# A hybrid decoder trunk on one core: whole-array transposes for DeltaNet's meta rows, and GLA score products in pieces of 24

## The chip, the cores and the metric

One core of a Trainium2 chip runs the whole program. The metric is device time in microseconds, the median over runs; less is better. TensorE (PE) multiplies matrices, VectorE (DVE) and ScalarE (ACT) work element by element, GpSimd (POOL) helps, and SyncE (SP) issues most of the transfers. Each engine takes its instructions in the order in which the program lists them.

## The reference

The reference is one layer of a language model with three token mixers side by side, for 512 tokens of width 2048 and 16 learned meta tokens ahead of them:

```
h    = pad(rms_norm(concat(meta, x), norm_w))
proj = h @ w_in                                # 2048 x ~7600 columns, split among three mixers
qkv  = silu(causal_depthwise_conv(dq, dk, dv))
o_dn  = gated_delta_rule(l2norm(q), l2norm(k), v, decay, beta)   # 6 heads x 128, chunked
o_gla = gla(q / 8, k, v, key-dim gate)                            # 5 heads, dk 64, dv 128
o_fox = softmax(q k^T / sqrt(128) + c_t - c_s, causal) v          # 5 heads x 128
each branch: times silu(z), the first two after a head norm
out  = rms_norm(x + concat(o_dn, o_gla, o_fox) @ w_out, final_norm_w)[:, 16:]
```

All of it is in float32. In GLA the score of query i and key j has a decay for each of the 64 key channels, `exp(g_i - g_j)`.

## The kernel before, in words

**Data and stages.** Tokens lie along the free axis, 16 meta tokens first (T = 528). Large products are made from operands split exactly into two parts (`hi`, `lo`), three products for each. The stages follow one another on TensorE:

1. The input projection. Nearly all of it runs as 18 pairs of 128-column blocks, each pair as seven products instead of eight (a Strassen-like scheme). `loads` fetches the weights of a pair as four tiles `a`, `sums` adds them on VectorE into `s` and back into `a`, `operand` splits each into `hp` (ScalarE) and `lp` (VectorE), `mm_pair` multiplies into the banks `px`, and `evac_pair` and `store` bring the result into the tile `u`. Pairs of DeltaNet's dk, dv and dq alternate with pairs of the other two mixers.
2. For each dk, dv and dq head, `conv` writes the convolved row into `cv`, and `token_rows` (line 725) turns it, so that tokens lie on partitions: four 128x128 transposes into one PSUM bank (`pkdk`, `pkdv`, `pkdq`), ScalarE's copies out of it into `u` (for dk after a pass of squares), a store; then, for dk and dv, a further transpose of the 16 meta columns into the same bank (line 742), ScalarE's one or two operations on it into `cv`, and a store into `kms` or `vms`. The further transpose overwrites what the copies read, so it waits for them. After it, bank, row `cv` and, with both heads of the pair done, tile `u` are given back.
3. DeltaNet, GLA and forgetting attention (Fox), woven into the last 16 single blocks of the input projection (`pbgq`, `pbgz`, `pbfq`, `pbfz`), which fill TensorE while the mixers wait for other engines.
4. The output projection (`po`, `ps`, `pz`) and the last norm.

**GLA's score products.** The 128x128 block of scores is cut in levels s = 64, 32, 16, 8, 4, 2, 1, 0. The levels go in four groups, (64, 32), (16, 8), (4, 2), (1, 0), for each of three pairs of heads (the third has one head). `level_operands` makes for each level a decayed key `kx` and query `qx` on VectorE and ScalarE. They lie in two sets of buffers, which come free when the products of the group are out. `gla_levels` (line 1377) lists the products of a group: 24 for (64, 32) and 64 for each of the others, in the third pair 12 and 32. They are small (64 rows by 64 or 32 columns) and write the banks `pss`. The list is handed to the planner in pieces of `CH` products (line 1401).

**The planner.** What runs when is worked out while the program is built. Every step is a generator (a chain) that yields operations; `Weave` keeps a clock for each engine from a table of costs, and lists the operations in the order in which its clocks let them start. Each engine then runs in that order. Chains have a priority, and on TensorE a slack in us, added to the time at which their operation is ready: 3.0 for `token_rows` (priority -0.1, line 854), 0.25 by default; the main stream of products has priority 0.25 (line 2047). On its clock a transpose costs 0.11 us and a small product 0.028.

TensorE's operations are of two classes. `light` are those with few columns, rows or weights (line 189). At a change of class the clock adds 0.1 us into light and 0.2 us back (`emit`, line 262). Which class is to come is settled by these lines, where `ran` is the time in the present class; after that, an operation of the wanted class that is ready on the clock is taken ahead of the one that priority and slack would choose:

```
op.light = key == "P" and (n < 64 or ins[0].shape[0] < P or ins[0].free_size() < P)
if self.mode:                                   # light now
    other = ran + (sum(o.dur for o in c[3]) if c[3][0].light else 0.0) > LIGHT      # 1.5
else:
    other = ran >= HEAVY                                                            # 1.5
kind = self.mode != other
if c[3][0].light != kind:
    like = [x for x in self.chains if ... x[3][0].light == kind and x[4] <= t + NEAR]   # 0.05
```

So a transpose of 16 columns is light, and one of 128 columns is not.

Of the kernel before, what the change touches and what calls it, by code (L numbers as in the profile page):

```python
# [18 lines left out]
P = 128  # L19
D = 2048  # L20
KT = D // P
NM = 16
# [66 lines left out]
NXP, SQP, NSL = -0.6, 0.0, 1.5  # L89
LP, LSL = 0.1, 1.0  # L90
EXTRA = ()
NOP, CH, CD = 0, 32, 32
WP, AOP, HDP = 1.0, -0.6, 0.0
EARLY_KP = (3, 4)
STK, KOS, OS0, OSN, OSP = (3, 4, 6, 7), 3, 1, 2, 0.1
# [267 lines left out]
def tile_hybrid_trunk(ctx, tc, xT, xtok, mtok, w_gate, w_first, w_in, w_out, consts, lmask, fin_w, out):  # L363
    nc = tc.nc
    ctx.enter_context(nc.allow_low_precision("operands are split exactly into two parts"))
    W = Weave(tc)
    V, A, G, PE, SP = (Engine(k, e) for k, e in zip("VAGPS", (nc.vector, nc.scalar, nc.gpsimd, nc.tensor, nc.sync)))
# [24 lines left out]
    ident = one((P, P), "ident")  # L392
# [332 lines left out]
    def token_rows(key, c, u):  # L725
        what, h = key
        g, j = divmod(h, H)
        blocks = [slice(b * P, (b + 1) * P) for b in range(NB)]
        dst, dstm, scale, acc_, ev = {"dk": (kds, kms, dl, nks, e_gate), "dv": (vps, vms, br, None, e_keys[g]),
                                      "dq": (None, None, None, nqs, e_gate)}[what]  # L730
        yield ev
        pk = yield Get(bank_s, f"pk{what}{h}", keep=2)
        yield [PE.transpose(pk[:, s], c[:, NM + s.start : NM + s.stop], ident) for s in blocks]
        if acc_ is not None:
            for b, s in enumerate(blocks):
                yield A.activation(u[:, s], pk[:, s], AF.Square, accum_out=acc_[:, b, h : h + 1])
        if dst is not None:
            for b, s in enumerate(blocks):
                yield A.activation(u[:, s], pk[:, s], AF.Copy, scale=scale[:, b, h : h + 1])
            yield SP.dma_start(out=dst[g].rearrange("p (b j) d -> p j b d", j=H)[:, j],  # L740
                               in_=u[:, :S].rearrange("p (b d) -> p b d", b=NB))
            yield PE.transpose(pk[:NM, :P], c[:, 0:NM], ident)
            m = c[:NM, P : 2 * P]
            if acc_ is not None:
                yield A.activation(m, pk[:NM, :P], AF.Square, accum_out=acc_[:NM, NB, h : h + 1])
            yield A.activation(m, pk[:NM, :P], AF.Copy, scale=scale[:NM, NB, h : h + 1])
            yield SP.dma_start(out=dstm[g][:, j], in_=m)
        bank_s.give(pk)
        row_s.give(c)
        sp_of(key).set()  # L750
        if what != "dv":
            {"dk": e_nk, "dq": e_nq}[what][h].set()
# [20 lines left out]
    pairs = [Pair(i) for i in range(len(PAIRS))]  # L773
# [68 lines left out]
    def store(p, n, u):  # L842
        yield VT(out=u, in0=u, in1=rstd, op=ALU.mult)
        key = p.keys[n]
        if key[0] in ("gz", "fz"):
            spill[key] = drp.tile([P, S], F32, name=f"sp{key[0]}{key[1]}")
            yield from silu_row(u[:, NM:], key, spill[key], True)
            sp_of(key).set()
        elif key[0] in CONV:
            c = yield Get(row_s, f"cv{p.i}{n}")  # L850
            yield from conv(u, key, c, u)
            if key[0] != "dv":
                yield spilled(key, c)
            W.go(token_rows(key, c, u), -0.1, f"rows{key[0]}{key[1]}", 3.0)
        else:
            yield spilled(key, u)
            sp_of(key).set()
# [68 lines left out]
    def give(t, *ss):  # L926
        for s in ss:
            if id(t) in s.held:
                s.give(t)
# [625 lines left out]
    def finish(i, z, s):  # L1555
        if i // 2 in ST:
            e_z[i].set((z, s))
            return
        if s:
            yield e_split  # L1560
        pools, keep = ((op_s, s), (KO, 3)) if s else (op_s, 0)
        hi = yield Get(pools, f"oh{i}", (P, S), F32R, keep)
        lo = yield Get(pools, f"ol{i}", (P, S), F32R, keep)
        dparts[i] = hi, lo
        if s is None:
            h_, l_ = (t.rearrange("p (b d) -> p b d", b=NB) for t in (hi, lo))
        else:
            h_, l_, z_ = hi, lo, z[:, :S]
        yield A.copy(h_, z_ if s else z)
        yield VT(out=l_, in0=z_ if s else z, in1=h_.bitcast(F32), op=ALU.subtract)  # L1570
        if s:
            s.give(z)
        for b in range(NB):
            oparts[i, b] = hi[:, b * P : (b + 1) * P], lo[:, b * P : (b + 1) * P]
        e_head[i].set()
# [156 lines left out]
    def phase_d():  # L1732
        yield e_c
        W.go(residual(), 0.0, "residual")
        for h in range(DN_HEADS):
            W.go(finish(h, gs[h // H].kd.rearrange("p (b j) d -> p j b d", j=H)[:, h % H], None), -0.05, f"split{h}")
        yield tuple(e_head[h] for h in range(DN_HEADS))
        e_split.set()
        for g in range(2):
            for q in range(3):  # L1740
                r_s.lend(gs[g].kd[:, 4 * q : 4 * q + 4, :].rearrange("p n d -> p (n d)"))
        for kp in ST:
            W.go(seven_heads(kp), HDP, f"heads{kp}")
        W.go(seven_loads(), -0.3, "sloads")
        W.go(seven_operands(), -0.45, "sops")
        yield tuple(e_z[i] for kp in ST for i in (2 * kp, 2 * kp + 1)) \
            + tuple(e_head[i] for kp in LATE for i in (2 * kp, 2 * kp + 1)) + (e_fin,)
        sweep()
        e_d.set()

    def sweep():
        w_s.move(d_s)
        f_s.move(d_s)
# [46 lines left out]

    def out_sums():
        for i, (cp, kp) in enumerate((cp, kp) for cp in range(2) for kp in ST):
            p, q = pairs[OS0 + OSN * i : OS0 + OSN * i + 2]
            yield p.done[1]
            t = osum[cp, ST.index(kp)]
            (a, b), (c, d) = (tuple(w_out[2 * cp + n, kp][:, k * S : (k + 1) * S] for k in range(2)) for n in range(2))
            for n, w in ((5, c), (7, d), (6, d), (4, b)):
                yield SP.dma_start(out=t[:, SUMS.index(n)], in_=w)
            for n, w, ev in ((5, a, p.done[6]), (7, c, p.done[7]), (6, t[:, SUMS.index(5)], q.done[1]),
                             (4, t[:, SUMS.index(6)], q.done[6])):  # L1810
                yield ev
                yield G.dma_start(out=t[:, SUMS.index(n)], in_=w, accum_op=ALU.add)
        e_osum.set()
# [4 lines left out]
    def seven_loads():  # L1818
        for s in SEV:
            for i, (n, kp) in enumerate((n, kp) for n in ORDER for kp in ST):  # L1820
                    if i == 6:
                        yield tuple(e_head[2 * kp] for kp in ST)
                    t = yield Get((r_s, d_s) if i > 5 or s.cp else r_s, f"w{s.cp}{kp}{n}", (P, S), F32,
                                  (0, KR) if i > 5 or s.cp else 0)
                    sm = osum[s.cp, ST.index(kp)]
                    raw = {1: (0, 0), 2: (0, 1), 3: (1, 1)}.get(n)
                    src = w_out[2 * s.cp + raw[0], kp][:, raw[1] * S : (raw[1] + 1) * S] if raw else sm[:, SUMS.index(n)]
                    yield SP.dma_start(out=t, in_=src)
                    s.src[kp, n].set(t)

    def seven_operands():
        yield e_d
        for s in SEV:
            for n in ORDER:
                if n == ORDER[NOP]:
                    yield tuple(e_head[2 * kp] for kp in ST)
                for kp in ST:
                    src = yield s.src[kp, n]
                    hi = yield Get(d_s, f"wh{s.cp}{kp}{n}", (P, S), F32R)
                    lo = yield Get(d_s, f"wl{s.cp}{kp}{n}", (P, S), F32R)  # L1840
                    yield A.copy(hi, src)
                    yield VT(out=lo, in0=src, in1=hi.bitcast(F32), op=ALU.subtract)
                    give(src, r_s, d_s)
                    s.op[n, kp].set((hi, lo))
# [37 lines left out]
    def residual():  # L1882
        for cc in range(4):
            for tb in range(4):
                yield OUT[cc][min(1 + tb // 2, len(OUT[cc]) - 1)].op
                acc[tb, cc] = yield Get(op_s, f"acc{cc}{tb}", (P, S), F32)
                yield SP.dma_start(out=acc[tb, cc], in_=xtok[tb * P : (tb + 1) * P, cc * 512 : (cc + 1) * 512])
            e_res[cc].set()
# [165 lines left out]
    W.go(phase_b(), 0.0, "phaseB")  # L2054
    W.go(phase_c(), 0.0, "phaseC")
    W.go(phase_d(), 0.0, "phaseD")
    W.go(final_weights(), 0.2, "finw")
    W.run()
# [57 lines left out]
```

## Time and profile before

| what | value |
|---|---|
| median of 3 runs | 963.39 us (963.23 to 964.7) |
| the profiled execution, its own time | 963.21 us |
| its span, first to last instruction | 961.4 us |
| mean granted TensorE clock | 0.997 |
| TensorE busy, by the record | 948.3 us |
| VectorE, ScalarE, GpSimd busy | 738.5, 581.2, 66.1 us |
| bytes moved | 167.20 MB, mean 174 GB/s |

Between the span and the execution's own time lie 1.8 us. The matrix records overlap: a product of 264 columns is recorded as 0.28 us long, and the next starts 0.12 us after it. So a time on TensorE is read from start to start and not from the length of a record. In the profile `x64` behind small products counts two records for each float32 product. All lines of the kernel carry the line of one helper (L285), so work is told apart by the names of tiles.

### The profile page before, as it was taken

The numbers are of one execution on the slowest core, as the hardware profiler recorded it, in microseconds if no ns is written. First come the engines' busy times: TensorE is split into PE (matmuls) and PEld (weight loads), VectorE is DVE, ScalarE is ACT, GpSimd is POOL, SyncE is SP. The second block draws the span as 40 slices with busy tenths as digits, with TensorE's granted clock in tenths as the row PEclk, the third lists the DMA queues.
The fourth block names the chain that finished last, engine by engine and source line by source line (L and its number), as shares of the span: only waits on it lengthen the run. The fifth ranks groups of instructions, "written<-read, shape, count | busy, mean of one in ns | idle before, by whom it ended". The sixth has DMA issues, their size and how long they took to land.

```text
span 961.4 us, 19098 instructions
## 1 busy us (share of the span) xinstructions
PE 948.3 (99%) x7283; PEld 844.6 (88%) x7283; DVE 738.5 (77%) x1308; ACT 581.2 (60%) x1243; POOL 66.1 (7%) x118
## 2 busy tenths in 40 slices
PE   9999999999999999999999999999999999999996
PEld 7888999999999999999987898878778878888885
DVE  7976888888888887888883665785765886887774
ACT  7855466757756575754432775848737756355445
POOL 0000101001101010110001110101010100000000
PEclk9999999999999999999999999999999999999998
DMA  9933647557786668783178545334323364565414
GB/s 348 367 121 132 162 136 219 163 183 197 198 239 151 208 150 224 183 241 93 67 255 297 167 95 172 135 101 146 117 95 111 130 213 154 195 230 174 151 59 176
DMA packets 92145, 167.20 MB, mean 174 GB/s; under 512 B 16253, under 2 KB 36477, under 8 KB 92052
## 3 DMA queue, kind: packets, MB, share of 16 engines
q1 hardware_dynamic: 87156, 157.31, 49.8%
q0 software_dynamic: 4608, 8.39, 6.3%
q8 instruction: 57, 0.93, 0.4%
q14 instruction: 36, 0.29, 0.1%
q10 hardware_dynamic: 288, 0.27, 0.1%
HBM read 142.33 MB, written 40.39 MB: 190 GB/s over the span
## 4 chain that ended last, share of the span: by engine, by line
PE 94%; DMA 2%; ACT 2%; DVE 1%; issue 0%; DVEq 0%; POOL 0%; SPq 0%; ACTq 0%; POOLq 0%
PE px L285 38%; PE po L285 10%; PE ps L285 8%; PE pbfz L285 6%; PE pz L285 6%; PE pbfq L285 5%; PE pbgz L285 5%; PE pbdz L285 2%; PE pks L285 2%; PE pfa L285 1%; PE pg L285 1%; PE pfw L285 1%; PE pss L285 1%; PE pbgq L285 1%; PE pgo L285 1%; DMA sc<-ab 1%
## 5 line engine op out<-in xcount | busy, mean ns | idle before, releaser
L285 DVE SCALAR_TENSOR_TENSOR lp<-a,hp 128x1024 fp32r<-128x1024 f32 x90 | 110.5, 1228 | 37.6 <-ACT hp L285 35.2
L285 ACT CAST hp<-a 128x1024 fp32r<-128x1024 f32 x90 | 94.5, 1049 | 72.4 <-PE px L285 45.4
L285 PE MATMUL px<-xh,hp 128*128 128x264 f32 x432 | 123.6, 286 | 0.0
L285 PE MATMUL px<-xh,lp 128*128 128x264 f32 x432 | 122.9, 285 | 0.0
L285 PE MATMUL px<-xl,hp 128*128 128x264 f32 x432 | 122.9, 285 | 0.0
L285 PE MATMUL px<-tah,hp 128*128 128x264 f32 x288 | 84.0, 292 | 0.0
L285 PE MATMUL px<-tbh,hp 128*128 128x264 f32 x288 | 82.5, 287 | 0.0
L285 PE MATMUL px<-tbh,lp 128*128 128x264 f32 x288 | 82.1, 285 | 0.0
L285 PE MATMUL px<-tah,lp 128*128 128x264 f32 x288 | 82.0, 285 | 0.0
L285 PE MATMUL px<-tbl,hp 128*128 128x264 f32 x288 | 81.9, 284 | 0.0
L285 PE MATMUL px<-tal,hp 128*128 128x264 f32 x288 | 81.8, 284 | 0.0
L285 PEld LDWEIGHTS px<-xh,hp 128*128 128x128 f32 x432 | 81.4, 188 | 0.0
L285 PEld LDWEIGHTS px<-xh,lp 128*128 128x128 f32 x432 | 81.3, 188 | 0.0
L285 PEld LDWEIGHTS px<-xl,hp 128*128 128x128 f32 x432 | 81.2, 188 | 0.0
L285 ACT CAST hp<-s 128x1024 fp32r<-128x1024 f32 x36 | 37.8, 1049 | 29.7 <-PE px L285 19.8
L285 PEld LDWEIGHTS px<-tbh,hp 128*128 128x128 f32 x288 | 54.3, 189 | 0.1
L285 PEld LDWEIGHTS px<-tbl,hp 128*128 128x128 f32 x288 | 54.3, 189 | 0.0
L285 PEld LDWEIGHTS px<-tah,hp 128*128 128x128 f32 x288 | 54.3, 188 | 0.1
L285 PEld LDWEIGHTS px<-tal,hp 128*128 128x128 f32 x288 | 54.3, 189 | 0.0
L285 PEld LDWEIGHTS px<-tah,lp 128*128 128x128 f32 x288 | 54.2, 188 | 0.0
L285 PEld LDWEIGHTS px<-tbh,lp 128*128 128x128 f32 x288 | 54.2, 188 | 0.0
L285 DVE SCALAR_TENSOR_TENSOR lp<-s,hp 128x1024 fp32r<-128x1024 f32 x36 | 44.0, 1222 | 8.4 <-ACT hp L285 8.4
(406 smaller groups left out, 2639.5 us busy)
## 6 DMA issues: line engine op xcount, KB each, us to landing
a<-in_w_in SPq DMA_DIRECT2D x72, 512.0 KB, 6.3
osum<-in_w_out SPq DMA_DIRECT2D x32, 256.0 KB, 6.2
o<-in_w_out SPq DMA_DIRECT2D x16, 512.0 KB, 3.6
kd<-osum SPq DMA_DIRECT2D x26, 256.0 KB, 3.6
kd<-in_w_out SPq DMA_DIRECT2D x21, 256.0 KB, 3.5
rgz<-in_w_in SPq DMA_DIRECT2D x10, 512.0 KB, 3.3
rfq<-in_w_in SPq DMA_DIRECT2D x10, 512.0 KB, 3.2
rfz<-in_w_in SPq DMA_DIRECT2D x10, 512.0 KB, 3.1
```

What stands on the lines that cost most here:

```text
L285: self.pin(op.call(*op.a, **op.kw))
```

## The change

In `token_rows` the transpose of the meta rows takes 128 columns of `cv` in place of 16 and writes all 128 partitions of the bank; ScalarE reads the same 16 of them as before. `CH` goes from 32 to 24, so the groups of 64 score products are handed over as 24, 24 and 16, and those of 32 as 24 and 8. `SPR` names a priority with the value that stood there, and `int()` around a product of two integers leaves it as it is.

```
-NOP, CH, CD = 0, 32, 32
+SPR = -0.45
+NOP, CH, CD = 0, 24, 32
...
-            yield PE.transpose(pk[:NM, :P], c[:, 0:NM], ident)
+            yield PE.transpose(pk[:, :P], c[:, 0:P], ident)
...
-        W.go(seven_operands(), -0.45, "sops")
+        W.go(seven_operands(), SPR, "sops")
...
-            p, q = pairs[OS0 + OSN * i : OS0 + OSN * i + 2]
+            p, q = pairs[OS0 + int(OSN * i) : OS0 + int(OSN * i) + 2]
```

## The prediction, made before the changed kernel ran

> **What bounds the kernel now.** I read the page first: which engine is busy, and what the chain that ended last is made of.
>
> ```profile
> PE 948.3 (99%) x7283; PEld 844.6 (88%) x7283; DVE 738.5 (77%) x1308; ACT 581.2 (60%) x1243; POOL 66.1 (7%) x118
> ...
> PE 94%; DMA 2%; ACT 2%; DVE 1%; issue 0%; DVEq 0%; POOL 0%; SPq 0%; ACTq 0%; POOLq 0%
> ```
>
> TensorE is busy for 948.3 us and is 94% of the chain. So an edit counts by what it adds to or takes from TensorE's own stream: time of its instructions, or pauses between them. Work moved on another engine counts only where TensorE then waits. The pauses that the profile names are in the view of waits, for TensorE alone:
>
> ```profile
> PE pkd L285 <- DVE gst L285: 1.0, 1, 1.0
> PE pfw L285 <- DVE ml L285: 0.5, 1, 0.5
> PE pkdv L285 <- ACT u L285: 0.5, 3, 0.2
> PE pvf L285 <- ACT fv L285: 0.4, 1, 0.4
> PE pks L285 <- ACT y L285: 0.3, 1, 0.3
> PE pss L285 <- DVE qx L285: 0.2, 1, 0.2
> ```
>
> One row, pkdv behind ACT u, is the first edit's own instruction: the transposes of the meta rows. The other five, 1.0 + 0.5 + 0.4 + 0.3 + 0.2 = 2.4 us, lie in the later stages.
>
> **First edit, the transposes of meta rows.** Before, each takes 16 columns of cv as weights; after, 128. There are six for dk and six for dv, twelve in all. The rows of weight loads by shape:
>
> ```profile
> L285 PEld LDWEIGHTS pkdk<-ident,cv 128*128 128x128 f32 x24 | 2.8, 141 | 0.0
> ...
> L285 PEld LDWEIGHTS pkdk<-ident,cv 128*16 128x16 f32 x6 | 0.5, 88 | 0.7 <-ACT u L285 0.2
> ```
>
> The load itself grows from 88 to 141 ns. What a transpose costs the stream is read from starts: from the product ahead of it to the second product behind it, less two intervals of a product (0.12 us each, as 185.01 to 185.13 shows). In the view in order of time, TensorE alone, first a group of four whole transposes (185 us), then three narrow ones: one that waited for nothing (188 us), the first of the twelve (124 us) and the last (361 us).
>
> ```profile
> 185.01 0.29 PE L285 MATMUL px<-tah,lp 128*128 128x264 f32 x1
> 185.13 0.60 PE L285 MATMUL pkdk<-ident,cv 128*128 128x128 f32 x4
> 185.49 0.37 PE L285 MATMUL px<-tah,hp 128*128 128x264 f32 x1
> 185.70 0.28 PE L285 MATMUL px<-tal,hp 128*128 128x264 f32 x1
> ```
>
> ```profile
> 188.01 0.28 PE L285 MATMUL px<-tbh,lp 128*128 128x264 f32 x1
> 188.13 0.27 PE L285 MATMUL pkdk<-ident,cv 128*16 128x128 f32 x1
> 188.16 0.37 PE L285 MATMUL px<-tbh,hp 128*128 128x264 f32 x1
> 188.37 0.29 PE L285 MATMUL px<-tbl,hp 128*128 128x264 f32 x1
> ```
>
> ```profile
> 123.75 0.29 PE L285 MATMUL px<-tah,lp 128*128 128x264 f32 x1
> ...
> 124.27 0.29 PE L285 MATMUL px<-tal,hp 128*128 128x264 f32 x1
> ```
>
> ```profile
> 360.68 0.28 PE L285 MATMUL px<-tah,lp 128*128 128x264 f32 x1
> 361.11 0.28 PE L285 MATMUL pkdv<-ident,cv 128*16 128x128 f32 x1 [0.15 <-ACT u L285]
> 361.14 0.37 PE L285 MATMUL px<-tah,hp 128*128 128x264 f32 x1
> 361.36 0.28 PE L285 MATMUL px<-tal,hp 128*128 128x264 f32 x1
> ```
>
> Four whole ones: 185.70 - 185.01 - 0.24 = 0.45 us, so 0.11 each. The narrow one at 188: 0.36 - 0.24 = 0.12. So narrow and whole cost TensorE the same. The first of the twelve costs 0.52 - 0.24 = 0.28, the last 0.68 - 0.24 = 0.44. Why so much more? ScalarE, in order of time, ahead of the two:
>
> ```profile
> 186.79 1.16 ACT L285 ACTIVATE u<-pkdk,dl 128x128 f32<-128x128 f32 x4
> 359.92 1.14 ACT L285 ACTIVATE u<-pkdv,br 128x128 f32<-128x128 f32 x4 [0.22 <-PE pkdv L285]
> ```
>
> At 188 ScalarE had read the bank by 187.95, before TensorE came. At 361 it was done at 361.06, and the transpose, which overwrites the bank, started 50 ns later: TensorE stood still for ScalarE's copies. Read so at all twelve, in order: 0.28, 0.21, 0.21, 0.11, 0.19, 0.15, 0.12, 0.11, 0.43, 0.43, 0.11, 0.43, sum 2.78 us, of which 12 x 0.11 = 1.3 is the transposes and the rest waits.
>
> Will those waits go? The planner puts a narrow transpose into its light class. In heavy mode, after 1.5 us of heavy work, it takes any light operation the moment it is ready by its clock, whatever slack the chain was given. A whole transpose is heavy. It then stands by its chain's slack of 3.0 and priority of -0.1 against the main stream's priority of 0.25, so it is placed some 2.65 us after the copies are due by the planner's clock. The groups of four are placed by that rule already, and the one above shows no wait. So I take 12 x 0.117 = 1.4 us (0.11 each and 0.01 for the change of shape, from 0.45 - 4 x 0.11) in place of 2.78: **-1.4 us**. Bounds: no wait goes, 0; no wait goes and the 53 ns longer load lies bare each time, +0.6 us; the best, every transpose at 0.11, -1.5 us.
>
> The Trainium skill, page "TensorE: Matmul & The Clock Gate", section "LDWEIGHTS (loading the stationary operand)", speaks against this edit: a load takes time by its columns, P / 1.2 ns, so 16 to 128 columns would add 93 ns, and by it, an estimate, the twelve would cost 1.1 us more if nothing hid them. The rows above have 53 ns more, and the group of four at 0.11 each leaves no bare load.
>
> What moves with it: each meta transpose comes some 2.6 us later, and with it ScalarE's two operations on it (dk) or one (dv), and on SP's queue the store of kms or vms. Behind that store, in order, stand weight loads; and the bank, the row cv and the tile u are given back later. The bank is one of eight, and the group's chain ends far from its readers, so these cost nothing while weights come early enough (second rival).
>
> **Second edit, pieces of 24.** A group of score products has 64 (pairs 0 and 1, three groups each), 32 (pair 2, three groups), or 24 and 12. Groups of 24 or less stay one piece. What a piece costs, in order of time:
>
> ```profile
> 639.48 0.40 PE L285 MATMUL pbfz<-xl,hbfz 128*128 128x512 f32 x1
> 639.72 0.40 PE L285 MATMUL pbfz<-xh,lbfz 128*128 128x512 f32 x1
> 640.04 0.76 PE L285 MATMUL pss<-qx,kx 64*32 64x32 f32 x64
> 640.73 0.50 PE L285 MATMUL pbfz<-xh,hbfz 128*128 128x512 f32 x1
> 641.07 0.40 PE L285 MATMUL pbfz<-xl,hbfz 128*128 128x512 f32 x1
> ```
>
> x64 are 32 products, two records each. From the big product before (639.72) to the second after (641.07): 1.35 us. Less two intervals of a big one (639.72 - 639.48 = 0.24) and the small products' own 0.57 (up to the first big one, 640.73 - 640.04 = 0.69, less 0.12 from the last small one to the big one): about 0.30 us for going into small products and out again. So the number of stretches matters, not the number of pieces. The planner's rule for a light stretch is 1.5 us: a piece of 32 is 0.1 + 32 x 0.028 = 1.0 on its clock, a second would make 1.9, so now each group of 64 is two stretches of 32. A piece of 24 is 0.77, a second makes 1.44, and 16 more 1.89: two stretches, 48 and 16. Groups of 32 become 24 + 8 at 1.0: one stretch as before. The count stays: **0 us**. Bounds: each group of 64 breaks into three stretches, 6 x 0.30 = +1.8 us; or each last stretch joins another, -1.8 us (but the next group's operands are made in buffers that come free only when this group's pieces are out, so I see nothing to join). A second piece right behind the first needs its operands 1.6 us sooner; the one wait on qx above prices that at 0.2 each, +1.2 us if all six meet it.
>
> The Trainium skill, page "TensorEngine Tiling (Array Packing)", section "Key Properties", says that changing the tiling mode drains TensorE. For the score products the trace agrees (0.30 us). For the 128x16 transposes it does not: 0.12 us at 188 is a whole one's price.
>
> **Third, SPR and int().** -0.45 and 2 are the values as before: nothing.
>
> **The order of everything behind.** The planner's clock charged 0.1 + 0.2 us of mode change for each narrow transpose: 3.6 us that go from its TensorE clock, and the order after that stage is drawn anew by it. The five late waits (2.4 us) may go, or as many more come: -2.4 to +2.4 us; no row tells a sign, so 0.
>
> **Sum.** The profiled execution took 963.21 us, 0.18 below the median of 963.39. 963.4 - 1.4 + 0 + 0 = 962.0 us, 0.14% less: within the 0.2% (1.9 us) that a measurement of this kernel tells from no change.
>
> **Rivals.**
> *The new order also loses late waits*: gst 1.0, ml 0.5 and fv 0.4 gone: 962.0 - 1.9 = 960.1. For it: each is a single event, due to the order of one moment. Against: nothing in the edits aims there.
> *Late weights, the slower side.* Rows of phase one, vector engine, TensorE and SP's queue:
>
> ```profile
> 370.24 1.23 DVE L285 SCALAR_TENSOR_TENSOR s<-a,a 128x1024 f32<-128x1024 f32 x1 [2.24 <-DMA a<-in_w_in]
> 371.38 0.42 DVE L285 TENSOR_TENSOR u<-u,px 128x264 f32<-128x264 f32 x1
> 371.72 1.22 DVE L285 SCALAR_TENSOR_TENSOR lp<-a,hp 128x1024 fp32r<-128x1024 f32 x1
> ```
>
> ```profile
> 374.95 0.29 PE L285 MATMUL px<-tbh,lp 128*128 128x264 f32 x1
> ```
>
> ```profile
> 364.86 0.38 SPq L285 DMA_DIRECT2D vms<-cv x1
> 365.33 0.84 SPq L285 DMA_DIRECT2D a<-in_w_in x2
> ```
>
> The load stands right behind vms, VectorE waited 2.24 us for it, and lp was ready at 372.94 for a product at 374.95: 2.0 us of lead. Were vms 2.6 us later and the load with it, TensorE would lack 0.6 us; with the lead used up in full as the delays add, up to 2.6. At six conv pairs: 6 x 0.6 = 3.6 to 6 x 2.6 = 15.6; near the low end, since the trace shows no product waiting there: 962.0 + 3.6 = 965.6. It decides from 3.3 / 6 = 0.55 us each. Against: ScalarE's part was done at 361.8 and vms went out 3 us later, behind other transfers.
> *The transposes still follow right on the copies*: 963.4.
> *Three stretches a group*: 962.0 + 1.8 = 963.8.
> *A drain at every change of shape* (the rule of the Trainium skill's page "TensorEngine Tiling (Array Packing)", above), priced by the score products: 12 x 0.30 = 3.6 less, 959.8. Against: all twelve together cost 2.78.
> *The new order brings waits*: 962.0 + 2.4 = 964.4.
>
> **How the numbers follow.** The forecast 0.42 (its small terms put 0.06 of that below 961.5, the bound of faster), better order 0.27, drain 0.03, no effect on the waits 0.08, three stretches 0.05, worse order 0.07 (0.03 of it beyond 965.3), late weights 0.08. Faster 0.06 + 0.27 + 0.03 = 0.36; slower 0.08 + 0.03 = 0.11; same 0.53. The range leaves out the far ends of better order and late weights: 959.2 to 965.0; the forecast alone has 961.2 to 963.0 (1.5 saved and 0.7 of waits less, or 0.4 saved).
>
> **What would show it.** Right: twelve more transposes of 128*128, none of 128*16, no row of pkdv behind ACT u, each at 0.11 to 0.12 us between products, about 2.6 us after the copies; score products in stretches of x96 and x32, as many stretches as before. Wrong: stretches of x48 three to a group; new rows of px behind DVE or DMA at 120 to 380 us; a sum of TensorE's waits after 520 us that differs from 2.4 by more than 1.5.

## The result: 0.47% slower, and the profile after

| | before | changed |
|---|---|---|
| median | 963.39 us (9 runs, 962.5 to 964.99) | 966.86 us (9 runs, 965.29 to 971.1) |
| profiled execution, its span | 963.21, 961.4 | 966.72, 964.6 |

The ratio is 1.0047, with a 95% interval of 1.0036 to 1.0058: slower, by 3.5 us between the medians and 4.5 us by the ratio. The forecast was 962.0 (959.2 to 965.0).

The page of the changed kernel (busy time of each engine, then the chain that ended last):

```profile
PE 947.8 (98%) x7283; PEld 845.1 (88%) x7283; DVE 739.4 (77%) x1308; ACT 580.7 (60%) x1243; POOL 68.5 (7%) x118
...
PE 93%; DVE 2%; ACT 2%; DMA 1%; issue 1%; SPq 0%; DVEq 0%; POOL 0%; ACTq 0%; POOLq 0%
```

TensorE is as busy as before (947.8 against 948.3 us), the span is 3.2 us longer: most of the added time is in pauses. Where, the view by stretches tells; its columns are length, busy time of PE, PEld, DVE, ACT and POOL, each with its instructions, then the granted TensorE clock (1.00 is full speed), the DMA share and GB/s. First before, then after:

```profile
0.00:500.00 500.00, 498.41 (x3686) 476.70 (x3687) 417.72 (x552) 313.71 (x558) 37.41 (x61) 1.00 0.65 191
500.00:560.00 60.00, 59.83 (x662) 49.72 (x660) 33.63 (x90) 30.38 (x72) 6.84 (x11) 1.00 0.68 222
560.00:760.00 200.00, 197.29 (x1891) 161.90 (x1890) 137.41 (x386) 132.22 (x395) 20.63 (x44) 1.00 0.39 125
```

```profile
0.00:500.00 500.00, 498.16 (x3690) 477.16 (x3691) 416.64 (x549) 312.85 (x558) 38.31 (x61) 1.00 0.64 191
500.00:560.00 60.00, 56.12 (x597) 44.68 (x597) 27.69 (x68) 23.12 (x43) 6.32 (x10) 0.97 0.64 209
560.00:760.00 200.00, 196.82 (x1912) 164.26 (x1912) 141.49 (x401) 136.70 (x419) 21.24 (x43) 1.00 0.39 127
```

Between 500 and 560 us TensorE pauses 60 - 56.12 = 3.9 us, before 0.2. This is the start of DeltaNet, where the changed lines do not stand. Single products say the same: the last `px` starts 0.9 us earlier than before, the last `pbgz` (at 711.4 us) 4.0 us later, and the last `pz`, near the end, 4.2 us later. So behind 711 us hardly anything more is lost. The first rows of the view of waits name the pauses:

```profile
PE pm L286 <- DVE uc L286: 2.2, 2, 1.2
PE pm L286 <- issue: 1.5, 1, 1.5
...
PE pkd L286 <- DVE gst L286: 1.0, 2, 0.6
PE pss L286 <- DVE qx L286: 0.5, 2, 0.3
PE pss L286 <- issue: 0.5, 1, 0.5
```

"issue" is time in which the engine waited for nothing that the profile shows. Neither of the two pm rows was among the five late waits of the prediction. The view of before has a row that belongs to the first: the handover was just in time already.

```profile
PE pm L285 <- DVE uc L285: 0.2, 1, 0.2
```

**The handover.** DeltaNet's triangular inverse is made on VectorE (`ot<-ab`), stored (`sc<-ab`, SP's queue), and read back for two groups of heads as `xc`; VectorE transposes `xc` into `uc`; then `levels` hands TensorE four lists `pm` of 32x32 products, 24 and 48 for each group, and `pn` follows. In the kernel before, at least six products of 512 columns (`pbgz`, `pbfq`) stand between any two lists. In the changed kernel the two groups' first lists follow on each other directly, and six such products stand ahead of each second list. VectorE before and after, in order of time:

```profile
520.31 0.58 DVE L285 STREAM_TRANSPOSE uc<-xc 128x384 f32<-128x384 f32 x1 [3.74 <-DMA xc<-sc]
...
523.40 0.58 DVE L285 STREAM_TRANSPOSE uc<-xc 128x384 f32<-128x384 f32 x1 [1.04 <-DMA xc<-sc]
```

```profile
525.15 0.58 DVE L286 STREAM_TRANSPOSE uc<-xc 128x384 f32<-128x384 f32 x1 [3.87 <-DMA xc<-sc]
527.28 0.58 DVE L286 STREAM_TRANSPOSE uc<-xc 128x384 f32<-128x384 f32 x1 [1.56 <-DMA xc<-sc]
```

The first `uc` is 4.8 us later. The inverse on VectorE now starts at 470.2 instead of 412.6 and its last step starts 2.7 us later, at 510.0 instead of 507.3; behind it, on SP's queue, `xc<-sc` goes out at 519.04 instead of 515.32, and the transfer takes the rest. Which choice of the planner moved the inverse, no run here shows. TensorE, after:

```profile
524.39 0.40 PE L286 MATMUL pbgz<-xh,lbgz 128*128 128x512 f32 x1
525.78 0.95 PE L286 MATMUL pm<-uc,an 32*32 32x32 f32 x48 [1.00 <-DVE uc L286]
527.91 1.25 PE L286 MATMUL pm<-uc,an 32*32 32x32 f32 x48 [1.19 <-DVE uc L286]
529.10 0.80 PE L286 MATMUL pbfq<-xh,hbfq 128*128 128x512 f32 x1
...
530.12 0.63 PE L286 MATMUL pbfq<-xh,lbfq 128*128 128x512 f32 x1
530.54 0.63 PE L286 MATMUL pbfq<-xh,hbfq 128*128 128x512 f32 x1
...
536.53 0.18 PE L286 MATMUL pm<-xc,m 32*32 32x32 f32 x1 [1.49 <-issue]
```

Before, the two groups' first lists started at 520.94 and 528.27, and the second waited for nothing; now both wait, 2.1 us apart. Behind the pauses the products of 512 columns start every 0.43 us instead of 0.23: the granted clock had fallen. The view by stretches has 0.50 from 528.3 to 531.7 and 1.00 on either side, which is 3.4 x 0.50 = 1.7 us more:

```profile
527.00:528.30 1.30, 0.39 (x24) 0.39 (x26) 1.02 (x2) 0.71 (x2) 0.00 (x0) 1.00 0.92 302
528.30:531.70 3.40, 3.40 (x42) 2.55 (x35) 1.94 (x5) 2.44 (x4) 0.00 (x0) 0.50 0.95 291
531.70:534.00 2.30, 2.30 (x102) 1.91 (x102) 0.54 (x1) 2.21 (x5) 0.41 (x1) 1.00 0.99 401
```

The third pause, 1.49 behind "issue", has no engine to wait for. In the DMA queues of the stretch from 534.2 to 536.5 there is one packet of kind instruction, q8, and none from 526 to 534.2; the second line is of the whole page:

```profile
q8 instruction: 1, 0.02, 2.4%
```

```profile
q8 instruction: 57, 0.93, 0.4%
```

0.93 MB in 57 packets is 16 KB each. The one here started at 534.29, and TensorE went on at 536.53, 2.2 us later: the row reads as if it had run out of instructions, and e10 and e13 below test that. The other runs bear it out: of TensorE's 19 waits for issue of over 0.25 us in all the traces (the first 100 us left out), 15 ended 2.2 to 2.5 us after such a packet had started, and three more 2.7 to 3.0 us after one; the last, e10's `pn` below, ended 0.4 us after one. The Trainium skill's page "Runtime: NRT & Kernel Launch", section "Terms", says that an engine's instruction memory is refilled in blocks of 16 KiB; the trace agrees on the size, and the row above shows what a block costs that comes late.

**The two edits themselves** did what the prediction said, in the main. The groups by shape have whole transposes alone, thirty for each of dk and dv, and one pkdv still waits for ScalarE:

```profile
L286 PE MATMUL pkdv<-ident,cv 128*128 128x128 f32 x30 | 5.4, 278 | 0.3 <-ACT u L286 0.3
L286 PE MATMUL pkdk<-ident,cv 128*128 128x128 f32 x30 | 5.2, 272 | 0.0
```

Score products, in order of time, stand as x96 and x32 in most groups. The x64 and x32 at 647 and 648 us are one stretch of 96, with a wait for qx inside:

```profile
646.98 0.76 PE L286 MATMUL pss<-qx,kx 64*32 64x32 f32 x64 [0.21 <-DVE qx L286]
648.06 0.55 PE L286 MATMUL pss<-qx,kx 64*32 64x32 f32 x32 [0.33 <-DVE qx L286]
650.15 0.36 PE L286 MATMUL pss<-qx,kx 64*32 64x32 f32 x32
```

### The profile page after: what moved, and what is told of

Its sections match the earlier page's. It is cut to its first block, busy times and chain, and to the rows that moved or that the text cites. A ratio compares the mean times of both kernels' runs of the same rounds, so it can differ in the third digit from the quotient of the medians.

```text
span 964.6 us, 19064 instructions
## 1 busy us (share of the span) xinstructions
PE 947.8 (98%) x7283; PEld 845.1 (88%) x7283; DVE 739.4 (77%) x1308; ACT 580.7 (60%) x1243; POOL 68.5 (7%) x118
## 4 chain that ended last, share of the span: by engine, by line
PE 93%; DVE 2%; ACT 2%; DMA 1%; issue 1%; SPq 0%; DVEq 0%; POOL 0%; ACTq 0%; POOLq 0%
PE px L286 38%; PE po L286 9%; PE ps L286 8%; PE pbfq L286 6%; PE pbfz L286 6%; PE pz L286 6%; PE pbgz L286 4%; PE pbdz L286 2%; PE pbgq L286 2%; PE pks L286 2%; PE pfa L286 1%; PE pg L286 1%; PE pfw L286 1%; PE pss L286 1%; DMA sc<-ab 1%
```

## The experiments

Ratios are to the kernel before, of runs on the same chip, with 95% intervals.

### One edit alone

**e1_transposes** has the changed kernel's transposes with `CH = 32`, **e2_pieces** has `CH = 24` with the narrow transposes.

> The transposes alone: all of the change but CH, which stays 32. Theory 'order' (the loss lies in the order that the planner draws after its clock has lost the twelve mode changes, at DeltaNet's start, where pm stands right behind the landing of the inverse): 965.5 to 967.5 us; pm waits for DVE uc about 2 us in all, as after, and the granted clock drops near 0.5 for 2 us behind it. Rival 'pieces' (the loss lies with CH = 24): 961.5 to 963 us.

> CH = 24 alone; the transposes stay 16 columns wide. Everything ahead of the score products stands in the order of the kernel before. Theory 'order': within 1 us of before, 962.5 to 964.5; pm waits 0.2 us for uc as before; a stall inside a stretch of 48 products may cost up to 0.7. Rival 'pieces': 965.5 us or more, with the loss between 620 and 800 us.

Measured: e1 974.67 us, 1.0114 (1.0101 to 1.0128); e2 975.87 us, 1.0129 (1.0115 to 1.0143). Both forecasts for e1 missed. e2's time is in its rival's range, but its loss lies behind 800 us and not between 620 and 800. Each edit alone costs 11 to 12 us, and both together 3.5 to 4.5: they do not add. With e1's transposes, 24 gains 6.5 to 7.8 us against 32 (by the ratios and by the medians); with the narrow ones it loses 12.3. In e1 the start of DeltaNet loses 2.1 us of TensorE's time (57.72 busy from 500 to 560 where before has 59.83), 3.1 us of pauses sit behind the mixers' end, and behind either the clock stood at 0.50 (528.0 to 534.8 and 862.5 to 865.9), which is 5.0 us more:

```profile
PE ps L286 <- ACT wh L286: 1.7, 1, 1.7
PE ps L286 <- DVE wl L286: 1.4, 1, 1.4
```

In e2 the start is untouched (59.76 busy); there the order of GLA against Fox flips, GLA's last head is out early (pgo 790.5 instead of 808.3), and TensorE stands for Fox's softmax:

```profile
PE pfa L286 <- ACT fp L286: 7.8, 4, 6.4
PE pfw L286 <- DVE ml L286: 1.9, 2, 1.3
```

Behind the longest of these pauses, 6.4 us, the clock stood at 0.50 until 814.6; for the 5.2 us in which TensorE was busy there that is another 2.6 us. So the pieces show no cost of their own up to 707 us (the last `pbgz` starts 1.0 us earlier than before) and lose 12 us by the order that they draw.

### The width or the order?

`light` is what the planner reads. **e3_whole_as_light** transposes 128 columns and books them as light, so the order is that of before; **e4_narrow_as_heavy** transposes 16 and books them as heavy, so the order is that of e1.

```
 e3:  tr = PE.transpose(pk[:, :P], c[:, 0:P], ident);      tr.light = True
 e4:  tr = PE.transpose(pk[:NM, :P], c[:, 0:NM], ident);   tr.light = False
```

> The transposes take 128 columns on the chip, but the planner books them as light, so that every engine's order is that of the kernel before, instruction for instruction; CH = 32. It shows what the width alone costs. Theory 'order': 963.4 within 0.7 us; the twelve still wait for ScalarE as before, 2.6 to 3.0 us in all. Rival 'width' (a whole transpose costs TensorE more): 964.5 to 967 us.

> The transposes take 16 columns as before, but the planner books them as heavy, so that every engine's order is that of the transposes-alone kernel, instruction for instruction; CH = 32. It has the order without the width. Theory 'order': the time of the transposes-alone kernel within 0.7 us, 965.5 to 967.5, with the same wait of pm for uc. Rival 'width': back at 963.4 or below.

Measured: e3 964.32 us, 1.0006 (0.9998 to 1.0015); e4 973.51 us, 1.0113 (1.0093 to 1.0133). By the medians the width costs nothing that can be told from zero (e3 lies between its two forecasts); the order is nearly all of e1's loss.

### Can the planner be told?

In **e5_uc4_p24**, **e6_uc4_p32** and **e7_uc4_p64** the planner books `uc` as ready 4 us later (`tv.lat += 4` on the VectorE transpose), with whole transposes and pieces of 24, 32 and 64. **e8_pad** is e1 with 0.3 us more on the planner's clock for each meta transpose (`tr.dur += 0.3`), what the narrow ones had been charged for the change of class.

> The changed kernel, pieces of 24, and one number on the planner's clock: the transpose uc of the inverse is booked as ready 4 us later, so TensorE gets other work until then. Nothing that runs is added or left out. Theory 'handover' (TensorE reaches pm before the inverse has landed, because the planner's clock lost the 3.6 us that it used to charge for the twelve mode changes): the waits of pm at 520 to 540 us fall from 3.7 us to under 0.7, the granted clock stays at 1.00 there, TensorE is busy for 59 us or more of 500 to 560; 963 to 966 us. Rival 'width or pieces': 966 us or more, with the waits gone and the time not back.

> The transposes alone (pieces of 32), with uc booked 4 us later as in the run before this. Theory 'handover': the 11 us that the transposes alone cost, tail included, come from the late start of DeltaNet; 963 to 966 us, within 1 us of the kernel with pieces of 24, since the size of a piece by itself costs nothing. Rival 'two losses' (the 5 us that TensorE waits at the seven products near 860 have a cause of their own): 968 to 971 us.

> The changed kernel with uc booked 4 us later and CH = 64, so that a group of score products is one piece. Six stretches fewer, at 0.30 us each by the rows of the kernel before: theory 'handover', with the order of GLA and Fox drawn anew: 958 to 963 us, faster than both kernels. Rival 'late heads' (Fox ends late and its last head stands behind the splits on VectorE, as with pieces of 24 alone): 968 us or more.

> The transposes alone (128 columns, heavy, pieces of 32), each booked at 0.41 us in place of 0.11, so that the planner's TensorE clock has the 12 x 0.3 us again that the narrow ones were charged. Theory 'handover': the waits of pm at 520 to 540 fall from 2.1 us with the transposes alone to 1 us or less; 964 to 967 us. Rival 'the later transposes' (not the clock but their place, 2.65 us behind the copies, makes the inverse late): pm waits 2 us as with the transposes alone.

Measured: e5 971.59, 1.0086 (1.0068 to 1.0104); e6 972.7, 1.0116 (1.0092 to 1.0140); e7 967.04, 1.0036 (1.0023 to 1.0049); e8 966.2, 1.0029 (1.0018 to 1.0040). The first three missed (of their rivals, only e5's has the time in its range): the wait for uc is gone in each, but pm then waits for instructions (2.4, 1.3 and 2.1 us), and e5 and e6 have e1's waits of ps as well. e8 came as expected in time and brings some 8 us of e1's 11 back: no wait of pm for instructions, no wait of ps, one wait for uc of 1.4 (1 or less was expected). Its transposes are whole and booked as heavy, as e1's are, so that alone does not make e1's loss; the 3.6 us that the planner's clock had lost point to most of it. But each of these draws all of the later order anew, so none prices one wait.

### The order kept, one wait changed

For these the planner's book-keeping is left alone and only the issue is changed, so that every other instruction stands where it stood. **e11_again** makes the kernel before late: its first `uc` transpose is issued five times over. **e9_later** takes the changed kernel and issues its first lists behind more of the products of 512 columns. **e10_half** and **e12_half_before** issue the four lists with half the instructions, in the changed kernel and in the one before.

```
 e11:  for _ in range(1 + again): self.pin(op.call(*op.a, **op.kw))    # 4 for uc of group 0
 e9:   o.later = LATER[g] + 0.028 * (len(mm) - i)                       # LATER = 4, 6 us of TensorE's clock
 e10:  o.skip = n % 2
       if not n % 2:
           o.a = p3[lo_, n : n + 2, :], an[hi_, n, lo_], uc[hi_, n : n + 2, :]
```

> The kernel before, every engine's order kept, with VectorE's transpose of xc into uc for the first group done five times over in a row: uc is ready 4 x 0.58 = 2.3 us later, nothing else is changed. Theory 'the late handover alone makes the loss': pm <- DVE uc grows from 0.2 to about 2.5, with a stretch at half clock behind it, 965.5 to 967 us, the loss of the changed kernel without either of its edits. Rival 'a wait there is made up for by what follows': 963.4 to 964.3.

> The changed kernel with every engine's order kept but for the start of DeltaNet: on TensorE six of the products of 512 columns that stand behind the first two lists of levels now stand ahead of the first list, six between the two lists, and the second lists follow with five between them; ScalarE's copies of these lists keep their order. Theory 'the late handover is the loss': the waits pm <- DVE uc (2.2 us in the changed kernel) fall under 0.5, the stretch at half clock behind them (about 1.1 us) goes too, so 962.8 to 964.2 us, the time of before, if the 1.7 us in which TensorE waits for instructions at 535 stay; down to 962 if they go as well. Rival 'the loss sits in what the order does later, and the idle time at 525 is made up': 966 to 967.5, as the changed kernel.

> The changed kernel, its order kept, with half of the instructions in the four lists of levels: each product of 32 columns takes the 64 columns of its neighbour with it, by its own weights, and the neighbour's product is left out, so the same columns are written by 72 instructions instead of 144 (the neighbours' values are not those of the reference). Theory 'TensorE runs out of instructions': the issue stall of 1.67 us at 535 goes, TensorE's waits at 500 to 560 are 1.2 to 2 us less, 964.5 to 966 us with the wait for uc unchanged. Rival 'the stall is no matter of instructions (the clock or the operands)': it stays at 1.3 us or more and the time is 966 to 967.5 less what the shorter lists save, under 1 us.

> The kernel before, its order kept, with the same halving of the lists' instructions (the neighbours' products are left out). There is no issue stall and 0.2 us of waiting for uc to remove, and the lists take 5.1 us instead of 5.9 by the two profiles. Theory 'the 4 us that the halving gave the changed kernel were the waits for instructions and the clock behind them': 962.2 to 963.4. Rival 'they were the shorter lists': 958.5 to 960.5.

**e11: 968.6 us, 1.0046 (1.0031 to 1.0061).** The late handover alone, with neither edit, makes a loss as large as the changed kernel's:

```profile
PE pm L286 <- DVE uc L286: 2.5, 1, 2.5
```

Its profiled execution took 966.52 us at a mean clock of 0.997, which is the pause and little more; the executions at 0.991 to 0.993 took 969.7 to 970.7. The changed kernel's do much the same: 965.3 to 966.7 at 0.997, 969.0 and 971.1 at 0.991 and 0.993 (but 970.3 at 0.995). The pause costs its length, and in some executions as much again in clock.

**e9: 967.2 us, 1.0036 (1.0024 to 1.0048).** The theory missed; the time is in the rival's range, though the loss is still at DeltaNet's start and not in what follows. The wait for uc is gone, and nothing is won. The waits from 500 to 560, and a stretch:

```profile
PE pm L311 <- issue: 2.6, 1, 2.6
PE pks L306 <- DVE zz L306: 0.2, 1, 0.2
```

```profile
534.80:541.60 6.80, 6.80 (x48) 5.65 (x48) 2.39 (x8) 4.18 (x8) 0.00 (x0) 0.50 0.00 0
```

The lists now stand closer together, TensorE runs out of instructions for 2.6 us, and the clock that follows takes 6.8 x 0.50 = 3.4 us.

**e10: 962.87 us, 0.9987 (0.9979 to 0.9996)**, 4 us less than the changed kernel by the medians, more than the 1 to 2.4 us that were expected, and below the one before, though with values left out. **e12: 963.06 us, 0.9998 (0.9989 to 1.0006).** So the shorter lists are worth nothing where nothing stalls, and the 4 us were stalls and the clock behind them. e10's waits from 500 to 560:

```profile
PE pm L287 <- DVE uc L287: 1.2, 2, 0.9
PE pks L287 <- DVE zz L287: 0.5, 2, 0.3
PE pn L287 <- issue: 0.5, 1, 0.5
```

The clock stays at 1.00. The wait for uc is a microsecond shorter too, because the second `xc` landed earlier: its transpose starts at 525.38 (525.47 in e13) where the changed kernel's profile has 527.28. The changed kernel's own profile is the odd one: its second transpose starts 2.1 us behind the first, in e9, e10, e13, e14 and e16, with the same order up to there, 1.1 to 1.2. Why that transfer was slower there, nothing here shows; so some 1 of the 4 us may be the transfer's.

### With all values kept

In the second lists half of the products can go: one quarter is the transpose of another (VectorE makes it), one is read by nothing. **e13_tr**, **e14_later_tr** and **e15_tr_before** are the changed kernel, e9 and the kernel before with that edit. **e16_second** drops the unread quarter alone, and moves the second group's first list behind the next six products.

```
 e13:  for o in mm[1::2]: o.skip = 1          # 48 of 144 products; VectorE: l1[32:64] <- l1[0:32] transposed
 e16:  for o in mm[3::4]: o.skip = 1          # 24 products;  LATER = 0, 3
```

> The changed kernel, its order kept; in the second lists of levels the 24 products of the lower half rows are not made on TensorE: for the first quarter VectorE transposes l1's rows 0 to 31 into rows 32 to 63 (the product xc,m1 is the transpose of the product m1,xc), and rows 96 to 127 are read by nothing. So 48 of the 144 products of the two groups go, about 2.0 us of 4.0 on TensorE by the rows of the kernel before, and all values stay. Theory 'instructions run out in dense lists': the issue stall of 1.5 at 535 goes or falls under 0.5, the wait for uc (2.2) and the half clock behind it stay: 963 to 964.5 us. Rival 'the stall stays': 964.5 to 965.5.

> The same edit on the kernel whose first lists stand later (967.2 us). Theory 'wait for uc and wait for instructions are the whole loss': neither is left (under 0.8 in all between 500 and 560), the clock stays at 1.00 there, 960 to 962 us, below the kernel before. Rival 'the order behind it loses something else': 963 or more.

> The same edit on the kernel before, its order kept: 2.0 us of TensorE's work go where nothing waits: 961 to 962.2 us. If VectorE's transpose, which stands in the chain of levels, comes late for the lists of l64, 962.5 to 964.

> The changed kernel, every engine's order kept, but for two things: the second group's first list of levels (24 products) stands behind the next six products of 512 columns on TensorE instead of right behind the first group's, and the 12 products of each second list whose rows 96 to 127 nothing reads are left out (24 in all, about 0.5 us at 20 ns each; l1 is copied without these rows, all values stay). No cover of a later list is moved. Theory 'the start is the whole loss': the second wait for uc (1.2) goes, the first (1.0) stays, the pause is too short for the half clock (it kept 1.00 after pauses of 0.9 in e10 and e13), and the denser middle list keeps up to 1 us of waiting for instructions: 962.3 to 964. Without the wait for instructions too: 962. Rival 'pauses only move on': 965.5 or more.

**e13: 964.05 us, 1.0009 (1.0000 to 1.0017)**: the time is as expected, and 2.8 us of the loss come back, but in part by luck. The wait for instructions is gone, as the theory said. The wait for uc of 2.2 and the half clock were expected to stay, and are 1.0 and none; pn now waits 0.9 for ACT uf. Of the whole execution's waits, the longest is now elsewhere:

```profile
PE pss L291 <- issue: 1.6, 1, 1.6
```

**e15: 964.35 us, 1.0017 (1.0003 to 1.0031).** Missed: by the interval, fewer products made the kernel before a little slower. GLA's score products met a refill that they had not met before, and e13 and e14, with the same products gone, meet it too (1.6 and 0.9 us at 796 and 799):

```profile
795.40 0.32 PE L290 MATMUL pss<-gqT,gkT 64*32 64x32 f32 x15 [1.19 <-issue]
```

**e14: 967.16 us, 1.0033 (1.0020 to 1.0047), and e16: 967.05 us, 1.0041 (1.0026 to 1.0057).** Both theories missed, and both times lie in their rivals' ranges. In e16 the second wait for uc is gone; a wait for instructions and one for `uf` stand in its place. The waits, and the clock after them:

```profile
PE pbfq L316 <- issue: 1.7, 1, 1.7
...
PE pm L316 <- DVE uc L316: 1.1, 1, 1.1
...
PE pn L316 <- ACT uf L316: 1.0, 1, 1.0
```

```profile
534.80:541.50 6.70, 6.02 (x34) 4.89 (x35) 2.21 (x10) 4.32 (x9) 0.00 (x0) 0.50 0.07 24
```

e14 has one pause instead (pn behind ACT uf, 3.5 us) and the same 3.4 us of clock. Moving one list moved the pause to the next link of the chain xc, uc, pm, l1, uf, pn. No version beat the kernel before with its values kept. What stays open is where the stream has to stand so that neither the refill nor the chain is met; of the orders here only that of the kernel before has it.

## Why the prediction was wrong, point by point

- **The transposes, -1.4.** The mechanism held, and the size came out smaller. All thirty are whole, the one shown for 188 us still costs 0.12, and it stands 2.0 us behind ScalarE's copies (186.89 to 188.93; forecast 2.65). Read from starts as the prediction read them, the twelve cost 1.98 us in place of 2.78, so 0.8 less: nine cost 0.11 to 0.12, and three still wait (0.18, 0.19 and 0.59, the last behind ACT u at 349.5). e9 and e16, with the same order there, have 1.82. By the whole stage, from the first px to the last, the changed kernel's profile gained 0.4 us, and the profiles of e9, e10, e13, e14 and e16 1.0 to 1.6. So the changed kernel's own profile lies at the low end; part of its difference is px behind DVE u, 0.3 at 372.6, which the prediction had listed as a sign against it.
- **The load of weights by columns**, the rule against the edit from the Trainium skill's page "TensorE: Matmul & The Clock Gate", section "LDWEIGHTS (loading the stationary operand)", is not settled by e3's time: the twelve longer loads cost 0.7 us by the medians, between -0.2 and 1.4, so that rule's 1.1, an estimate, and zero both fit. The rows of e3's profile are the finer measure. Where a transpose waits for ScalarE's copies, the whole one costs 0.04 to 0.07 us more than the narrow one in the same place (0.33 against 0.28 at 124 us, 0.48 against 0.43 at 296), apart from one with a wait of its own of 0.6; where it waits for nothing, 0.00 to 0.01 (0.12 for either at 188). That is less than the 0.09 of that rule. So the prediction's bound, in which the 53 ns lie bare where no wait goes, was put rightly.
- **Pieces of 24, 0.** Stretches of 48 and 16 came as worked out (with one group in a single stretch). The zero holds for the pieces as far as these runs show, and not for their effect: e2 shows 12 us by the order of GLA against Fox. That the handing over of a list is itself an input to the planner was said for the transposes and forgotten here.
- **The order of everything behind, -2.4 to +2.4, sign 0.** This is the step that failed. It was bounded by the pauses that the trace of before names, as if a new order could only add or take as many again. e1, e2 and e4 show what it can do: 11 to 12 us from one switch, and 6.5 to 7.8 back from the other. What was put at 0 measured, in the changed kernel's profile, 3.7 us more of pauses between 500 and 560 us and 1.7 us of slower clock behind them. With the transposes' -0.8 that is 4.6 us, near the 3.5 to 4.5 by which the kernel got slower. And the list of waits in the prediction stopped short: the view has three more late rows of 0.2, and pm behind uc is one of them. A wait of 0.2 is a chain that arrives just in time; this chain feeds four lists, and 2.3 us of lateness there cost 0.46%, 4.4 us (e11).
- **The rivals.** The slower one named late weights in phase one. None came that cost more than 0.5 us. A drain at every change of shape (959.8) falls with e3, whose transposes change no shape and which is not faster. The worse order (964.4) had the right cause and half the size (2.4 of the 4.9 us by which the forecast missed); nothing in the prediction had a price for a pause beyond its length, neither clock nor refills.
- **What would show it wrong** was put rightly: a new row of px behind DVE u at 372, and waits of TensorE after 520 us that make some 6.5 us in place of 2.4.

## What to carry to other kernels

Where an order is worked out from a table of costs, an edit that changes a booked cost or the length of a list is an edit to the whole program behind it: price it by redrawing the order (one width with the other's booking, as e3 and e4, splits the two), not by the rows of the edited instructions. Read the smallest wait rows on long chains as margins of zero, and ask what a few microseconds of lateness would cost there. And judge a pause by what follows it: here a slower clock came behind most of the longer ones, and lists of small products moved out of the way of one wait met a late refill of instructions or the next link of the chain, so that moving one list only moved the pause.

## What the runs showed of the hardware

- **A pause is repaid in clock.** With pauses of at most 0.9 us at a time at 524 to 535 (e10, e13) the granted clock stayed at 1.00. With 1.0 and 1.19 a microsecond apart it fell to 0.50 for 3.4 us (changed kernel, 1.7 us lost), with 2.6 in one (e9), or 1.65 and 0.97 (e16), for 6.8 us (3.4 and 3.0 lost), and with 6.4 (e2), from within the pause on, for 10.2 us. It is not the same in every execution: e11's pause of 2.47 kept 1.00 in its profile, while its other executions went down to a mean of 0.991. The Trainium skill's page "TensorE: Matmul & The Clock Gate", section "What's actually happening", puts the fall to half after an idle window of about 3.4 us, free-running. The depth agrees (0.50), and so does the length, in that the stretches at 0.50 last 3.4 us or two or three times that. But the window need not be idle: in the 3.4 us ahead of the changed kernel's fall TensorE stood still for 2.1 us, and between the pauses it ran small products.
- **TensorE can run out of instructions.** Refills are 16 KB, and TensorE mostly went on 2.2 to 2.5 us after the packet of one had started. In or shortly behind lists of small float32 products it stood for 0.3 us (e11) to 2.8 us (e4). Whether it does hangs on where the refill falls: taking 48 products away at 525 us made a new stall of 1.19 us at 795 (e15).
